# Causal masks written first into their PSUM banks, two query blocks sharing a bank, in the forgetting attention of a hybrid trunk

## The chip, the core and the metric

The kernel runs on one core of one Trainium2 chip. A core has five engines, each with its own in-order queue: TensorE (PE, with the weight load shown as PEld), VectorE (DVE), ScalarE (ACT), GpSimd (POOL) and SyncE (SP), which issues the DMAs. TensorE writes to PSUM, which has eight banks of 512 float32 columns on each of 128 partitions; VectorE and ScalarE read it there. The metric is the device time of one execution in microseconds (us), lower is better. A difference of about 0.2% (4.7 us) is what a measurement of this kernel can tell from no change.

## The reference

The reference is a two-layer trunk on 1024 frames of 1024 channels: a layer of forgetting attention (FoX), a layer of gated linear attention, each followed by a SwiGLU. The change touches the attention only:

```python
log_f = jax.nn.log_sigmoid(f_logit + b_f)
cum = jnp.cumsum(log_f, axis=1).transpose(0, 2, 1)
for blk in range(S // Q_BLOCK):                      # 8 blocks of 128 queries
    qs, qe = blk * Q_BLOCK, (blk + 1) * Q_BLOCK
    logits = jnp.einsum('bqhd,bkhd->bhqk', q[:, qs:qe], k[:, :qe]) * scale
    logits = logits + cum[:, :, qs:qe, None] - cum[:, :, None, :qe]
    mask = (qs + jnp.arange(Q_BLOCK))[:, None] >= jnp.arange(qe)[None, :]
    p = jax.nn.softmax(jnp.where(mask, logits, -inf), axis=-1)
    outs.append(jnp.einsum('bhqk,bkhd->bqhd', p, v[:, :qe]))
```

There are 16 heads of 64 channels. Query block qb attends to the first (qb + 1) * 128 keys, and the causal mask cuts only the last 128 of them, the diagonal block.

## The kernel before, in words

The attention works on pairs of heads p = 0 to 7, in each on a head a = 0 or 1, and in each head on four pairs of query blocks, g = 0 to 3, in the order `ORDER = (0, 3, 1, 2)`; query block qb is 2g + qi. `scores(u)` computes one such unit (p, a, g). It cuts the keys of a query block into pieces of at most 512 columns: one piece for qb 0 to 3 (128, 256, 384 and 512 wide), and two for the others (384 + 256, 512 + 256, 512 + 384, 512 + 512). That makes 12 pieces and 8 masks a head.

For each piece TensorE writes two matmuls into a PSUM tile: `Qs` with `K1` (L1260) and `Qs` with `KL` (L1261), in which float32 operands are split in a high and a low part. The piece that ends on the diagonal gets a third one (L1263), 128 columns wide: the bfloat16 identity times `maskb`, a constant block, which adds the mask. VectorE then reads the piece out of PSUM (L1266), adds the cumulated gates, writes it to the tile `lp` and keeps the running minimum of each row in `st`; a second piece starts from the first one's minimum. ScalarE takes the exponential of the whole row and its sum (L1270), VectorE the reciprocal (L1271), GpSimd multiplies (L1272).

The PSUM tiles of the pieces come from a ring of two banks, `sr`, b0 and b1 in turn (`sr, tr, orr, pj = ps_rings(2, 3, 1, 2)`). A piece can be written only when VectorE has read the piece that had its bank before.

`outputs` then transposes the probabilities on TensorE (L1292, tiles `t`), ScalarE and VectorE split them in a high and a low part (L174, L175, tiles `pt`), and TensorE multiplies with V (L1304, L1306, tiles `o`). A unit's `outputs` follows the next unit's `scores`. `weave` interleaves all that with the projections of the next head pair (tiles `qk` and `vps`, L305 to L307), or in the last pair with the output projection (`fo`), by the costs that each step yields. A scheduler then fixes each engine's order when the program is built, and adds the waits; the engines run in that order. VectorE also computes parts of the conditioning vector there (tiles `acc0`, L503 and L505), whose weights come by DMA.

## Time and profile before

| what | value |
|---|---|
| median of 3 runs | 2363.45 us (2361.98 to 2363.59) |
| span of the profiled execution | 2360.5 us, from its first to its last instruction |
| time of the profiled execution outside its span | not listed; its span lies 2.95 us below the median of the runs |
| attention, all of its score pieces | about 97 us to 605 us of the span |
| TensorE busy | 2339.7 us, 99% of the span |
| mean granted TensorE clock | 0.994 |

The rows shown below give for each group of instructions or for each run of equal instructions a start in the span, a duration, the engine, the line of the kernel, the operation, and its output and inputs; at the end, in brackets, how long the engine sat idle before it and what ended that. The duration of a matmul is its time from start to end in a pipeline: what it takes from TensorE's time is the distance from its start to the next one's start. A weight load (PEld) runs beside the matmul before it.

### The profile page before, as it was taken

How to read it: one execution, taken by the hardware profiler on the slowest of the kernel's cores; microseconds unless marked ns; L12 is line 12 of the kernel's file. 1: busy time of each engine (PE TensorE's matmuls, PEld its weight loads, DVE VectorE, ACT ScalarE, POOL GpSimd, SP SyncE). 2: the span in 40 equal slices, each digit the busy share in tenths (PEclk: the TensorE clock that was granted, in tenths of full speed). 3: DMA queues.
4: the chain of work that ended last, by engine and by line, in shares of the span. 5: the costliest groups of instructions: out<-in, count | busy, mean ns of one | idle time of the engine just before them, and what ended most of it. 6: DMA issues, size and time to landing. Idle time of an engine off the chain costs nothing. (4 is left out here: it accounts for less than half of the span.)

```text
span 2360.5 us, 35758 instructions
## 1 busy us (share of the span) xinstructions
PE 2339.7 (99%) x12208; PEld 1992.7 (84%) x12208; DVE 1791.0 (76%) x2996; ACT 1122.5 (48%) x2186; POOL 1101.5 (47%) x993
## 2 busy tenths in 40 slices
PE   8999999999999999999999999999999999999999
PEld 7888888888888888888888898898888888888888
DVE  6578787886688888885788765668787777876787
ACT  6556566575453343345324644444453433345326
POOL 1334444533355666653363531345446665643262
PEclk8999999999999999999999999999999999999999
DMA  8423333332435545457665543554434544457664
GB/s 265 145 79 113 105 121 95 121 126 99 134 100 173 189 161 170 159 185 259 225 224 170 147 130 93 148 180 169 143 114 163 165 152 147 157 197 259 227 198 150
DMA packets 348719, 375.00 MB, mean 159 GB/s; under 512 B 25500, under 2 KB 286776, under 8 KB 348536
## 3 DMA queue, kind: packets, MB, share of 16 engines
q1 hardware_dynamic: 348536, 372.72, 48.2%
q8 instruction: 96, 1.57, 0.3%
q14 instruction: 87, 0.71, 0.1%
HBM read 275.56 MB, written 97.06 MB: 158 GB/s over the span
## 5 line engine op out<-in xcount | busy, mean ns | idle before, releaser
L175 DVE TENSOR_TENSOR o_s<-xv_s,o_s 128x512 fp32r<-128x512 f32 (+1 forms) x376 | 322.4, 862 | 54.5 <-ACT o_s L174 52.9
L174 ACT CAST o_s<-xv_s 128x512 fp32r<-128x512 f32 (+1 forms) x376 | 216.9, 587 | 290.5 <-PE p_b L307 239.1
L307 PE MATMUL p_b<-B,o_s 128*128 128x512 f32 x608 | 236.0, 389 | 0.0
L305 PE MATMUL p_b<-B,o_s 128*128 128x512 f32 x608 | 235.6, 390 | 0.4 <-DVE x L1637 0.4
L306 PE MATMUL p_b<-B,o_s 128*128 128x512 f32 x608 | 235.9, 389 | 0.0
L918 POOL TENSOR_TENSOR ex_s<-xv_s,xv_s 128x512 f32<-128x512 f32 (+1 forms) x64 | 90.5, 1414 | 285.1 <-DMA xv_s<-in_ffn_w_in_dram 118.8
L1272 POOL TENSOR_SCALAR lp_s<-lp_s,st 128x128 f32<-128x128 f32 (+7 forms) x128 | 98.1, 770 | 246.3 <-DVE st L1271 230.7
L305 PE MATMUL p_b<-T,o_s 128*128 128x512 f32 x480 | 186.9, 389 | 0.0
L306 PE MATMUL p_b<-T,o_s 128*128 128x512 f32 x480 | 186.8, 389 | 0.0
L307 PE MATMUL p_b<-T,o_s 128*128 128x512 f32 x480 | 181.2, 389 | 0.0
L305 PEld LDWEIGHTS p_b<-B,o_s 128*128 128x128 f32 x608 | 114.1, 188 | 24.5 <-DVE x L1637 1.0
L307 PEld LDWEIGHTS p_b<-B,o_s 128*128 128x128 f32 x608 | 114.1, 188 | 23.9
L306 PEld LDWEIGHTS p_b<-B,o_s 128*128 128x128 f32 x608 | 114.1, 188 | 23.5
L1270 ACT ACTIVATE lp_s<-lp_s,st 128x128 f32<-128x128 f32 (+7 forms) x128 | 99.4, 777 | 59.7 <-DVE st L1266 58.6
L920 POOL TENSOR_TENSOR xv_s<-ex_s,xv_s 128x512 f32<-128x512 f32 (+1 forms) x64 | 87.4, 1366 | 62.3 <-DVE o_s L175 60.0
L174 ACT CAST pt_s<-t_b 128x512 fp32r<-128x512 f32 (+1 forms) x160 | 79.7, 547 | 72.0 <-PE t_b L1292 71.4
L1637 DVE TENSOR_TENSOR ex_s<-ex_s,p_b 128x512 f32<-128x512 f32 x140 | 93.7, 681 | 19.6 <-PE p_b L307 19.5
L175 DVE TENSOR_TENSOR pt_s<-t_b,pt_s 128x512 fp32r<-128x512 f32 (+1 forms) x160 | 96.3, 630 | 15.7 <-ACT pt_s L174 15.1
L307 PEld LDWEIGHTS p_b<-T,o_s 128*128 128x128 f32 x480 | 90.1, 188 | 18.7
L305 PEld LDWEIGHTS p_b<-T,o_s 128*128 128x128 f32 x480 | 90.1, 188 | 18.6
L306 PEld LDWEIGHTS p_b<-T,o_s 128*128 128x128 f32 x480 | 90.1, 188 | 18.6
L246 POOL TENSOR_TENSOR w_l_s<-w__s,w_h_s 128x256 fp32r<-128x256 f32 x90 | 69.6, 801 | 76.7 <-ACT w_h_s L242 58.8
(1801 smaller groups left out, 7440.8 us busy)
## 6 DMA issues: line engine op xcount, KB each, us to landing
xv_s<-in_ffn_w_in_dram SPq DMA_DIRECT2D x176, 256.0 KB, 3.2
hid_B<-x SPq DMA_DIRECT2D x70, 512.0 KB, 2.9
ad_s<-in_ada_w_dram SPq DMA_DIRECT2D x384, 64.0 KB, 2.4
hid_T<-x SPq DMA_DIRECT2D x36, 512.0 KB, 2.9
xv_s<-in_ffn_w_out_dram SPq DMA_DIRECT2D x96, 192.0 KB, 5.0
ada_s<-in_ada_w_dram SPq DMA_DIRECT2D x96, 128.0 KB, 2.8
xv_s<-in_ffn_w_out_dram SPq DMA_DIRECT2D x40, 256.0 KB, 2.9
T2o<-hid_T SPq DMA_DIRECT2D x18, 512.0 KB, 8.5
```

Of the source, the lines that this page charges most:

```text
L174: nc.scalar.copy(hi, src)
L175: nc.vector.tensor_sub(lo, src, hi.bitcast(F32))
L246: (nc.gpsimd if i < 3 else nc.vector).tensor_sub(lo[:, cs], rw[:, cs], hi[:, cs].bitcast(F32))
L305: nc.tensor.matmul(ps, ah, bh, start=start, stop=False, skip_group_check=chain)
L306: nc.tensor.matmul(ps, ah, bl, start=False, stop=False, skip_group_check=chain)
L307: nc.tensor.matmul(ps, al, bh, start=False, stop=stop, skip_group_check=chain)
L918: nc.gpsimd.tensor_add(s1, a21, a22)
L920: nc.gpsimd.tensor_sub(a11, s1, a11)
L1270: nc.scalar.activation(lp, lp, AF.Exp, bias=mcur, scale=-1.0, accum_out=st[:, qi, 2:3])
L1272: nc.gpsimd.tensor_scalar(lp, lp, st[:, qi, 3:4], 1.0, op0=ALU.mult, op1=ALU.mult)
L1637: nc.vector.tensor_add(d, d if src is None else dest(G, src), ps)
```

## The change

In `scores`, the mask is now the first matmul into its PSUM tile, with `start=True`, and the pieces accumulate onto it. It is issued by a helper, `masks`, a piece by `piece`, and the exponential and what follows by `exps`. What the four pairs of query blocks do now:

- g = 0: one bank holds both query blocks (128 and 256 columns). One mask matmul of 256 columns, in two blocks at columns 0 and 256, is written first, then the piece of qb 0, then that of qb 1.
- g = 1: two banks as before; both masks stand in the program ahead of the first piece.
- g = 2: the first 384 columns of qb 4 as before; then one bank for the last 256 columns of qb 4 and the last 256 of qb 5, with one mask matmul of 256 columns ahead; then the first 512 columns of qb 5. So the two pieces of qb 5 are in the opposite order.
- g = 3: the same pieces as before, with the masks ahead of the second ones.

A head now has 6 mask matmuls in place of 8 (96 in place of 128 in all), 10 banks in place of 12, and the same 12 pieces. No transfer is added or removed; in the built order of SyncE's queue seven short stretches of DMA issues within the attention differ.

```diff
--- before.py
+++ after.py
@@ -1249,27 +1249,74 @@
         else:
             lps = [lpr([P, (2 * g + 1 + i) * P], F32, f"lp{p}{a}{g}{i}") for i in range(2)]
         st = sm.tile([P, 2, 4], F32, tag="st", bufs=4, name=f"st{p}{a}{g}")
-        for qi in range(2):
+        least = [[], []]
+
+        def masks(ps, at):
+
+            o_, m_ = ps[:, at[0]:at[0] + P], maskb
+            if len(at) == 2:
+                o_ = ps.rearrange("p (a b) -> p a b", b=at[1] - at[0])[:, :, at[0]:at[0] + P]
+                m_ = maskb.unsqueeze(1).to_broadcast([P, 2, P])
+            nc.tensor.matmul(o_, identb, m_, start=True, stop=False, skip_group_check=True)
+
+        def piece(ps, c0, qi, k0, k1, masked, last):
+
             qb = 2 * g + qi
-            qs, lp, Wd, mcur = psl(qb), lps[qi], (qb + 1) * P, 3e38
-            cuts = (0, 384, 640) if Wd == 640 else (0, Wd) if Wd <= HALF else (0, HALF, Wd)
-            for n_, (k0, k1) in enumerate(zip(cuts, cuts[1:])):
-                ps = sr([P, k1 - k0], F32, f"s{p}{a}{qb}{k0}")
-                early = u == (0, 0, 0)
-                diag = k1 == Wd
-                nc.tensor.matmul(ps, Qs[:, qs], K1[:, k0:k1], start=True, stop=False)
-                nc.tensor.matmul(ps, Qs[:, qs], KL[:, k0:k1], start=False, stop=not diag)
-                if diag:
-                    nc.tensor.matmul(ps[:, k1 - k0 - P:], identb, maskb, start=False, stop=True)
-                mnew = st[:, qi, n_:n_ + 1]
-                with tc.issue_after(v_last) if early else ExitStack():
-                    nc.vector.tensor_tensor_reduce(lp[:, k0:k1], ps, cm[:, k0:k1], 1.0, mcur,
-                                                   ALU.add, ALU.min, mnew)
-                mcur = mnew
-                yield max(0.22, 0.00085 * (k1 - k0))
-            nc.scalar.activation(lp, lp, AF.Exp, bias=mcur, scale=-1.0, accum_out=st[:, qi, 2:3])
+            o_, qs = ps[:, c0:c0 + k1 - k0], psl(qb)
+            nc.tensor.matmul(o_, Qs[:, qs], K1[:, k0:k1], start=not masked, stop=False, skip_group_check=masked)
+            nc.tensor.matmul(o_, Qs[:, qs], KL[:, k0:k1], start=False, stop=last, skip_group_check=masked)
+            got = least[qi]
+            mnew = st[:, qi, len(got):len(got) + 1]
+            with tc.issue_after(v_last) if u == (0, 0, 0) else ExitStack():
+                nc.vector.tensor_tensor_reduce(lps[qi][:, k0:k1], o_, cm[:, k0:k1], 1.0, got[-1] if got else 3e38,
+                                               ALU.add, ALU.min, mnew)
+            got.append(mnew)
+            return max(0.22, 0.00085 * (k1 - k0))
+
+        def exps(qi):
+            lp = lps[qi]
+            nc.scalar.activation(lp, lp, AF.Exp, bias=least[qi][-1], scale=-1.0, accum_out=st[:, qi, 2:3])
             nc.vector.reciprocal(st[:, qi, 3:4], st[:, qi, 2:3])
             nc.gpsimd.tensor_scalar(lp, lp, st[:, qi, 3:4], 1.0, op0=ALU.mult, op1=ALU.mult)
+
+        def bank_(n, nm):
+            return sr([P, n], F32, f"s{p}{a}{g}{nm}")
+
+        if g == 0:
+            ps = bank_(HALF, "")
+            masks(ps, (0, 256))
+            yield piece(ps, 0, 0, 0, P, True, False)
+            exps(0)
+            yield piece(ps, P, 1, 0, 2 * P, True, True)
+            exps(1)
+        elif g == 1:
+            p0, p1 = bank_(3 * P, 0), bank_(4 * P, 1)
+            masks(p0, (2 * P,))
+            masks(p1, (3 * P,))
+            yield piece(p0, 0, 0, 0, 3 * P, True, True)
+            exps(0)
+            yield piece(p1, 0, 1, 0, 4 * P, True, True)
+            exps(1)
+        elif g == 2:
+            ps = bank_(3 * P, 0)
+            yield piece(ps, 0, 0, 0, 3 * P, False, True)
+            ps = bank_(HALF, "")
+            masks(ps, (P, 3 * P))
+            yield piece(ps, 0, 0, 3 * P, 5 * P, True, False)
+            exps(0)
+            yield piece(ps, 2 * P, 1, 4 * P, 6 * P, True, True)
+            ps = bank_(HALF, 1)
+            yield piece(ps, 0, 1, 0, HALF, False, True)
+            exps(1)
+        else:
+            for qi in range(2):
+                ps = bank_(HALF, 2 * qi)
+                yield piece(ps, 0, qi, 0, HALF, False, True)
+                n_ = (3 + qi) * P
+                ps = bank_(n_, 2 * qi + 1)
+                masks(ps, (n_ - P,))
+                yield piece(ps, 0, qi, HALF, HALF + n_, True, True)
+                exps(qi)
         return lps
 
     def outputs(u, lps):
```

The lines of the mask and of the two matmuls of a piece are L1260, L1266 and L1267 in the changed kernel, VectorE's read is L1271, the reciprocal L1279, the transposes L1339, the products with V L1351 and L1353.

The scheduler's order of the two programs is the same before the attention and, apart from line numbers, after it on all five engines. In the order of the kernel before, 108 of the 128 masks are followed by a matmul with float32 weights that isn't a transpose, and 20 by a transpose. In that of the changed kernel all 96 are followed by such a float32 matmul, none by another mask (so the two masks of g = 1 don't stand side by side in TensorE's queue), and 19 of them come directly after a transpose.

The first place is TensorE's queue at the start of the third head pair (p = 2). `s2000` and `s2010` are the score tiles of qb 0 and qb 1 of the kernel before, `s200` is the shared one and `s2030` the next unit's first; `b0` and `b1` are the banks, `qk031` is a projection. Before:

```order
L1260 MATMUL s2000_b0_49_2479<-KA2_1690,QA2_1688 128x128 [waits DVE_49]
L1261 MATMUL s2000_b0_49_2479<-KLA2_1692,QA2_1688 128x128
L1263 LDWEIGHTS identb_72
L1263 MATMUL s2000_b0_49_2479<-maskb_84,identb_72 128x128
L305 MATMUL qk031_b7_18_2594<-h0h5_187,w384_h_s23_17_1953 128x512
L306 MATMUL qk031_b7_18_2594<-h0l5_188,w384_h_s23_17_1953 128x512
L307 MATMUL qk031_b7_18_2594<-h0h5_187,w384_l_s24_18_1954 128x512
L1260 MATMUL s2010_b1_50_2507<-KA2_1690,QA2_1688 128x256 [waits DVE_49]
L1261 MATMUL s2010_b1_50_2507<-KLA2_1692,QA2_1688 128x256
L1263 LDWEIGHTS identb_72
L1263 MATMUL s2010_b1_50_2507<-maskb_84,identb_72 128x128
```

In the changed kernel:

```order
L1260 LDWEIGHTS identb_72
L1260 MATMUL s200_b0_41_2463<-maskb_84,identb_72 128x2x128 [waits DVE_49]
L1266 MATMUL s200_b0_41_2463<-KA2_1682,QA2_1680 128x128
L1267 MATMUL s200_b0_41_2463<-KLA2_1684,QA2_1680 128x128
L305 MATMUL qk031_b7_18_2576<-h0h5_187,w384_h_s23_17_1943 128x512
L306 MATMUL qk031_b7_18_2576<-h0l5_188,w384_h_s23_17_1943 128x512
L307 MATMUL qk031_b7_18_2576<-h0h5_187,w384_l_s24_18_1944 128x512
L1266 MATMUL s2030_b1_42_2560<-KA2_1682,QA2_1680 128x512 [waits DVE_49]
L1267 MATMUL s2030_b1_42_2560<-KLA2_1684,QA2_1680 128x512
L1266 MATMUL s200_b0_41_2463<-KA2_1682,QA2_1680 128x256 [waits DVE_49]
L1267 MATMUL s200_b0_41_2463<-KLA2_1684,QA2_1680 128x256
```

One mask of 256 columns stands ahead of both pieces; the 512-column piece of the next unit has moved ahead of qb 1's piece, which now waits for VectorE (to have read qb 0's piece out of the same bank), and the mask itself carries the wait for the bank.

The second place is VectorE's queue at the end of the fifth head pair (p = 4), between the reads of qb 4 and those of qb 5 (tiles `lp4121`, `st412`). Before:

```order
L505 SCALAR_TENSOR_TENSOR acc0_s25_1_749<-ada043_s18_48_5093,c42_164,acc0_s25_1_749 128x256 [waits DMAHW6_49,DMAHW7_49,DMAHW1_49,DMAHW0_49]
L175 TENSOR_TENSOR pt4110_s51_96_4823<-t4110_b4_96_4818,pt4110_s51_96_4823 128x512 [waits Activation_49]
L505 SCALAR_TENSOR_TENSOR acc0_s25_1_749<-ada043_s18_48_5093,c42_164,acc0_s25_1_749 128x256 [waits DVE_49]
L1271 RECIPROCAL st412_4760<-st412_4760 128x1 [waits Activation_49]
L505 SCALAR_TENSOR_TENSOR acc0_s25_1_749<-ada043_s18_48_5093,c42_164,acc0_s25_1_749 128x256 [waits DVE_49]
L175 TENSOR_TENSOR pt4111_s48_97_4830<-t4111_b2_97_4826,pt4111_s48_97_4830 128x384 [waits Activation_49]
L1266 ISA lp4121_s47_63_4759,st412_4760<-s4150_b0_119_4803,cum9_s44_10_4058 128x512 [waits PE_49,Pool_49]
L1266 ISA st412_4760 128x1
L505 SCALAR_TENSOR_TENSOR acc0_s25_1_749<-ada043_s18_48_5093,c42_164,acc0_s25_1_749 128x256 [waits DVE_49]
L1321 TENSOR_TENSOR oT4_s52_5_4203<-o413_b5_38_4674,ot413_4755 64x256 [waits Activation_49]
L1266 ISA lp4121_s47_63_4759,st412_4760<-s415512_b1_120_4807,cum9_s44_10_4058,st412_4760 128x256 [waits DVE_49,PE_49]
```

In the changed kernel:

```order
L505 SCALAR_TENSOR_TENSOR acc0_s25_1_749<-ada043_s18_48_5051,c42_164,acc0_s25_1_749 128x256 [waits DMAHW6_49,DMAHW1_49,DMAHW7_49,DMAHW0_49,DVE_49]
L1279 RECIPROCAL st412_4722<-st412_4722 128x1 [waits Activation_49]
L505 SCALAR_TENSOR_TENSOR acc0_s25_1_749<-ada043_s18_48_5051,c42_164,acc0_s25_1_749 128x256 [waits DVE_49]
L175 TENSOR_TENSOR pt4110_s51_96_4783<-t4110_b4_96_4778,pt4110_s51_96_4783 128x512 [waits Activation_49]
L505 SCALAR_TENSOR_TENSOR acc0_s25_1_749<-ada043_s18_48_5051,c42_164,acc0_s25_1_749 128x256 [waits DVE_49]
L175 TENSOR_TENSOR pt4111_s48_97_4790<-t4111_b2_97_4786,pt4111_s48_97_4790 128x384 [waits Activation_49]
L505 SCALAR_TENSOR_TENSOR acc0_s25_1_749<-ada043_s18_48_5051,c42_164,acc0_s25_1_749 128x256 [waits DVE_49]
L1271 ISA lp4121_s47_63_4721,st412_4722<-s412_b0_99_4727,cum9_s44_10_4026 128x256 [waits PE_49,Pool_49]
L1271 ISA st412_4722 128x1
L1271 ISA lp4121_s47_63_4721,st412_4722<-s4121_b1_100_4768,cum9_s44_10_4026,st412_4722 128x512 [waits DVE_49]
L1271 ISA st412_4722 128x1
```

The reciprocal of qb 4 has moved ahead of a split of transposed probabilities (`pt4110`) and a step of the conditioning vector (`acc0`); the reads of qb 5 have moved together, the 256-column one ahead of the 512-column one, behind all four steps of `acc0`.

## The prediction

> **What bounds the kernel now.** I read the page first, then the attention's stretch alone (busy time by window), then what TensorE waited for in it.
>
> ```profile
> span 2360.5 us, 35758 instructions
> PE 2339.7 (99%) x12208; PEld 1992.7 (84%) x12208; DVE 1791.0 (76%) x2996; ACT 1122.5 (48%) x2186; POOL 1101.5 (47%) x993
> 97.00:605.00 508.00, 502.88 (x3218) 440.72 (x3217) 378.80 (x960) 304.03 (x647) 221.85 (x316) 1.00 0.34 105
> PE t_b L1292 <- POOL lp_s L1272: 2.7, 3, 1.8
> PE qk_b L305 <- DVE QB L842: 1.1, 2, 0.5
> PE s_b L1260 <- DVE st L1266: 0.4, 2, 0.3
> ```
>
> TensorE is busy for 503 of the attention's 508 us (the columns of the third row are TensorE, its weight load, VectorE, ScalarE, GpSimd, clock). What it waits for there is small, and the longest wait, 1.8 us, is for normalised probabilities. So TensorE's own work is the bound, and a matmul taken away is worth what it takes from TensorE's time, as long as no wait fills the hole. VectorE, at 379 of 508 us, has room on average, but not everywhere (below).
>
> **What a mask costs.** The group of the masks, and the weight load of an ordinary score matmul:
>
> ```profile
> L1263 PEld LDWEIGHTS <-identb x128: 95/96/146, 97.5 to 589.5; 128*128 128x128 bf16 x128
> L1263 PE MATMUL s_b<-maskb,identb x128: 229/230/330, 97.5 to 589.5; 128*128 128x128 bf16 x128
> L1261 PEld LDWEIGHTS s_b<-KLA,QA x96: 187/189/333, 97.4 to 559.4; 128*128 128x128 f32 x96
> ```
>
> 230 ns is a latency, and isn't taken from TensorE's time. The price is in the starts. First a mask ahead of a 512-column matmul, then one ahead of 256-column ones, then one ahead of transposes, and last two transposes without a mask:
>
> ```profile
> 193.03 0.40 PE L307 MATMUL qk_b<-h0h,w_l_s 128*128 128x512 f32 x1
> 193.26 0.39 PE L305 MATMUL qk_b<-h0h,w_h_s 128*128 128x512 f32 x1
> 193.49 0.22 PE L1260 MATMUL s_b<-KB,QB 128*128 128x128 f32 x1
> 193.55 0.27 PE L1261 MATMUL s_b<-KLB,QB 128*128 128x128 f32 x1
> 193.66 0.23 PE L1263 MATMUL s_b<-maskb,identb 128*128 128x128 bf16 x1
> 193.71 0.48 PE L306 MATMUL qk_b<-h0l,w_h_s 128*128 128x512 f32 x1
> 194.02 0.40 PE L307 MATMUL qk_b<-h0h,w_l_s 128*128 128x512 f32 x1
> ...
> 183.29 0.23 PE L1263 MATMUL s_b<-maskb,identb 128*128 128x128 bf16 x1
> 183.32 0.36 PE L305 MATMUL vps_b<-wv_0h_s,h0h 128*128 128x256 f32 x1
> 183.53 0.28 PE L306 MATMUL vps_b<-wv_0l_s,h0h 128*128 128x256 f32 x1
> 183.65 0.28 PE L307 MATMUL vps_b<-wv_0h_s,h0l 128*128 128x256 f32 x1
> ...
> 179.52 0.23 PE L1263 MATMUL s_b<-maskb,identb 128*128 128x128 bf16 x1
> 179.58 0.50 PE L1292 MATMUL t_b<-ident,lp_s 128*128 128x128 f32 x3
> 179.84 0.36 PE L305 MATMUL vps_b<-wv_4h_s,h0h 128*128 128x256 f32 x1
> 180.04 0.28 PE L306 MATMUL vps_b<-wv_4l_s,h0h 128*128 128x256 f32 x1
> ...
> 211.10 0.38 PE L1292 MATMUL t_b<-ident,lp_s 128*128 128x128 f32 x2
> 211.23 0.48 PE L306 MATMUL qk_b<-h0l,w_h_s 128*128 128x512 f32 x1
> 211.55 0.40 PE L1260 MATMUL s_b<-KB,QB 128*128 128x512 f32 x1
> ```
>
> A 512-column matmul takes 0.23 us (193.03 to 193.26), a 256-column one 0.12 (183.53 to 183.65). From the mask's start to the end of the next matmul's slot it is 0.36 (193.66 to 194.02) and 0.24 (183.29 to 183.53). So a mask takes 0.13 and 0.12 us, though only 0.04 to 0.05 pass until the next start: the rest shows as a longer slot of its successor, whose 189 ns weight load doesn't fit behind so short a matmul. I take 0.125. Two transposes take 0.45 - 0.23 = 0.22 (211.10 to 211.55 with a 512-column matmul), 0.11 each. So the mask ahead of three transposes takes 0.52 - 0.33 - 0.12 = 0.07.
>
> **The change part by part.** *Masks of before.* By the built order 108 masks are followed by a float32 matmul that is no transpose and 20 by a transpose: 108 x 0.125 + 20 x 0.07 = 14.9 us of TensorE's time.
>
> *Masks of after.* 64 of 128 columns, all ahead of a float32 score matmul: 64 x 0.125 = 8.0. The 32 of 256 columns have no row. Bounds: no dearer than two masks (0.25), and no cheaper than 0.12, the slot of a 256-column float32 matmul; I take 0.12, since such a slot already hides a float32 weight load (183.53 to 183.65). 32 x 0.12 = 3.8 (to 8.0). Sum 11.8, so the edit gives 3.1 us; at the dear end, 16.0, it costs 1.1.
>
> *Masks behind transposes.* 19 masks now follow a transpose. Between 193.49 and 194.02 three 128-column matmuls (K1, KL, mask) take 0.53 - 0.23 = 0.30, though the first has the next float32 load behind it (0.11) and so has the mask (0.125): about 0.06 is left for the middle one, whose successor is the mask with its 96 ns load. A transpose ahead of a mask may likewise take 0.06 in place of 0.11: 19 x 0.05 = 0.9, between 0 and 0.9. I take 0.9. TensorE's work falls by 4.0 us (4.0 to -1.1).
>
> The Trainium skill, "TensorE: Matmul & The Clock Gate", section "Back-to-back issue gap", has about 81 ns a matmul for a stream of loads and 128-column matmuls and 262 cycles, an estimated 109 ns, for 256 columns. By it the masks would fall from 128 x 81 = 10.4 us to 64 x 81 + 32 x 109 = 8.7, a gain of only 1.7 us. The rows above, with a float32 load behind the bfloat16 matmul, are dearer than its 81 ns, and I go by them.
>
> *Pieces, reads, exponentials.* Same numbers and widths; nothing is gained or lost in work. The first mask of a piece hides nothing new: it needs only constants and a free bank, and the score matmuls behind it would have waited for that bank. The masks of g = 1 are not neighbours in the built order, so they cost what single ones do. The seven stretches of DMA issues that differ go past waiting steps of their queue; DMA is 0.34 busy in the stage (the window's eighth number), and I cost them at nothing; if weights came late, TensorE's projections would wait.
>
> *The new waits.* The second piece in a shared bank waits for VectorE to have read the first, and behind it in TensorE's queue wait projections, transposes and products with V that need nothing of it. How far VectorE lags at worst: the 384-column piece of qb 4 at the end of the fifth head pair, and its read.
>
> ```profile
> 398.88 0.34 PE L1261 MATMUL s_b<-KLB,QB 128*128 128x384 f32 x1
> ...
> 408.63 0.55 DVE L1266 CUSTOM_DVE_ANT_0 lp_s<-s_b,cum_s 128x384 f32<-128x384 f32 x1
> ```
>
> Nearly 10 us. But in the built order the second piece mostly stands several us of other matmuls behind the first; in the first place shown with the change, three 512-column projections and a pair of 512-column scores, 5 x 0.23 = 1.15 us. Tightest are the ends of the head pairs, where the next unit's mask of 256 columns follows closely on the piece that holds its bank. How it stands there before:
>
> ```profile
> 531.06 0.23 PE L1263 MATMUL s_b<-maskb,identb 128*128 128x128 bf16 x1
> 531.54 0.33 PE L1260 MATMUL s_b<-KA,QA 128*128 128x128 f32 x1 [0.25 <-DVE st L1266]
> ...
> 530.79 0.69 DVE L1266 CUSTOM_DVE_ANT_0 lp_s<-s_b,cum_s 128x512 f32<-128x512 f32 x1
> 531.94 0.47 DVE L1266 CUSTOM_DVE_ANT_0 lp_s<-s_b,cum_s,st 128x256 f32<-128x256 f32 x1
> ```
>
> TensorE there already waits for a 512-column read (0.69 us, to 531.48). Afterwards it waits for a 256-column read (0.47) that can start only when the piece itself is done. Bounds for the six ends where TensorE has next to nothing between (the second to seventh head pair): from 0 (VectorE late anyway) to the whole read, 0.47, each. What the masks save inside these few us is lost too, since the chain read, exponential, reciprocal, normalising sets when TensorE goes on. I take 0.2 us for each of six, 1.2 us, between 0 and 2.8.
>
> *The sum.* -4.0 + 1.2 = -2.8 us. It is made against the profiled execution, whose span of 2360.5 lies 2.95 us below the median of the runs (what lies around the span isn't listed, and I carry it over): 2363.45 - 2.8 = 2360.6 us. After the attention the built order is unchanged, so that part should only shift.
>
> **The rivals.** *Slower: the shared bank.* VectorE's lag, not TensorE's work, could decide at the 32 second pieces. The rule of the Trainium skill, "PSUM — Partial Sum Buffer", section "PSUM bank collisions raise a hardware error", speaks for it: guard by bank, not by address, so one engine may not read one half while another writes the other half. The built order has such a wait at every second piece; no run here shows the error. The gain is gone at 4.0 / 32 = 0.125 us a piece, and the kernel is 0.2% slower from (4.0 + 4.7) / 32 = 0.27 us. With 0.4 us, about a 256-column read, it is 12.8 - 4.0 = +8.8: 2372. Against it: TensorE's waits for these reads (L1260 on L1266) are 0.4 us in all today.
>
> *Faster: the longest wait goes as well.* At the end of the fifth head pair TensorE stands still, and just afterwards runs at half clock:
>
> ```profile
> 412.04 0.23 PE L1263 MATMUL s_b<-maskb,identb 128*128 128x128 bf16 x1
> 414.09 0.55 PE L1292 MATMUL t_b<-ident,lp_s 128*128 128x128 f32 x3 [1.82 <-POOL lp_s L1272]
> ...
> 415.50:418.90 3.40, 3.40 (x16) 3.04 (x15) 2.81 (x10) 2.11 (x6) 1.09 (x2) 0.51 0.85 260
> ```
>
> The transposes wait for qb 4's probabilities. The built order moves the reciprocal that they need ahead of a split and a step of `acc0`, which should shorten the wait by about half. If wait and half clock (3.4 x 0.49 = 1.7 us) both went, that would be 1.8 + 1.7 = 3.5 us more than the 4.0: 2363.45 - 7.5 = 2356. Against it: the reads of qb 5 are now behind all four steps of `acc0`, and the mask of the next unit waits for one of them.
>
> *Nothing: the gain is swallowed.* If VectorE's chain sets the pace for the last third of each head pair, or if the merged mask costs as much as two, what TensorE saves comes back as waiting: between -1 and +2 us, say 2364.
>
> **How the numbers follow.** The forecast, 2360.6, has its own bounds at -4.0 (no new wait) and -0.3 (waits of 2.8 and no gain behind transposes): 2359.4 to 2363.1; since starts are read to 0.01 us, the price of 128 masks may be off by 1.3 us besides. It gets 0.35, the faster rival 0.27, the slower 0.23, nothing 0.15. Faster by over 0.2% (below 2358.7): 0.27 and 0.09 of the forecast, 0.36. Slower (above 2368.2): 0.23. Within: 0.26 of the forecast and the 0.15, 0.41. The range goes from 2355.5, the faster rival, to 2367.5, the lower part of the slower one; some 0.2 is left out, mostly above.
>
> **What would show it.** In the changed profile: 96 masks, the start distances of a merged mask and its successor together about 0.12 us above that successor's own slot; attention's stretch 2 to 4 us shorter and the rest unchanged; TensorE's waits on L1271 of some 1 us in all, at the ends of the head pairs. I am wrong if these waits reach 4 us, if the merged mask takes 0.2 us, or if half-clock stretches come or go.

## The result, and the profile after

The changed kernel takes 2371.93 us (median of 5 runs, 2369.98 to 2372.3) beside 2363.45 us (2361.82 to 2365.68): a ratio of 1.0031, 95% interval 1.002 to 1.0041, so 0.3% slower, by some 8 us. The forecast was 2360.6 and the range ended at 2367.5.

The first lines of the page of the changed kernel: span, then each engine's busy time, share of the span and instructions.

```profile
span 2370.5 us, 35659 instructions
PE 2342.6 (99%) x12176; PEld 1992.7 (84%) x12176; DVE 1788.6 (75%) x2996; ACT 1121.0 (47%) x2186; POOL 1101.1 (46%) x993
```

TensorE has 32 matmuls fewer and is busy 2.9 us longer. The busy share, 99% in both, shows nothing: a matmul at half clock counts as busy, and the waits that matter are a few us. So the stages were compared by starts of the same matmuls in two profiled executions of each kernel (the second ones are runs of the next section). "Attention" goes from the first score or mask matmul to the last product with V; the "head loop" is the stage of the gated linear attention from the first transpose of a finished output (tile `ogt`) to the first matmul of the output projection (tile `oc`). The last row is the time of the profiled execution itself.

| us | before | before, again | after | after, again |
|---|---|---|---|---|
| attention | 507.2 | 506.2 | 510.6 | 508.3 |
| from there to the head loop | 764.5 | 763.9 | 766.3 | 765.4 |
| head loop | 246.8 | 246.9 | 251.3 | 255.6 |
| from there to the end | 744.7 | 745.0 | 744.6 | 746.1 |
| time of the execution | 2362.3 | 2362.2 | 2372.3 | 2375.6 |

Between the means of the two pairs, the attention is 2.8 us longer, the way to the head loop 1.7, the head loop 6.6, the remainder 0.5 (11.6 in all; these four executions lie further apart than the medians, which differ by 8.5). About half of the loss (4.5 of 10.0 us between the first profiles, 6.6 of 11.6 between the means) lies in a stage that the change doesn't touch, 765 us behind it.

**In the attention.** TensorE's queue around a merged mask and, further on, around another one (start, duration, engine, line, operation):

```profile
192.69 0.28 PE L1260 MATMUL s_b<-maskb,identb 128*128 128x256 bf16 x1
192.72 0.31 PE L1266 MATMUL s_b<-KB,QB 128*128 128x128 f32 x1
192.87 0.28 PE L1267 MATMUL s_b<-KLB,QB 128*128 128x128 f32 x1
...
216.01 0.28 PE L1260 MATMUL s_b<-maskb,identb 128*128 128x256 bf16 x1
216.05 0.36 PE L1266 MATMUL s_b<-KB,QB 128*128 128x256 f32 x1
216.25 0.28 PE L1267 MATMUL s_b<-KLB,QB 128*128 128x256 f32 x1
216.37 0.40 PE L306 MATMUL qk_b<-h0l,w_h_s 128*128 128x512 f32 x1
```

From the merged mask to the end of its successor's slot pass 216.25 - 216.01 = 0.24 us, and the 256-column matmul behind takes 0.12: the merged mask costs 0.12 us, as much as one of 128 columns. (At all 17 places where a merged mask stands ahead of a 256-column matmul the two take 0.23 to 0.24 us.) To separate work from standing still, I gave every matmul between the two ends of the attention the usual distance to the next start for its kind between such neighbours (the 35th percentile over all traces of this study) and called the remainder stalls (what half clock costs is among them). Before: 490.6 us of work and 16.6 and 15.6 of stalls. After: 486.8 and 23.8 and 21.4. By this estimate TensorE's work fell by 3.7 us, and stalls took back 4.8 to 8.2. Its size hangs on which neighbours are counted: by the shape of the matmul before alone the work falls by 2.6 us, by the shapes of both neighbours by 5.4. That stalls grew holds in each.

What TensorE waited for in the changed kernel's attention (waiter, releaser: us in total, times, longest), and then how long its clock was halved; the columns of the last rows are TensorE, weight load, VectorE, ScalarE, GpSimd, granted clock, DMA share, GB/s:

```profile
PE t_b L1339 <- POOL lp_s L1280: 1.6, 2, 1.0
PE s_b L1260 <- DVE st L1271: 1.4, 3, 0.6
PE o_b L1353 <- DVE oT_s L1368: 1.3, 4, 0.4
PE qk_b L305 <- DVE QB L842: 1.2, 2, 0.7
PE o_b L1353 <- DVE pt_s L175: 1.1, 3, 0.5
PE s_b L1266 <- DVE st L1271: 0.6, 2, 0.3
PE t_b L1339 <- DVE pt_s L175: 0.5, 2, 0.4
```

```profile
415.50:418.90 3.40, 3.06 (x9) 2.04 (x8) 2.62 (x9) 1.91 (x6) 1.02 (x2) 0.50 0.92 290
476.90:480.30 3.40, 2.95 (x8) 2.38 (x9) 1.54 (x7) 0.87 (x4) 1.85 (x4) 0.50 0.38 141
1514.60:1518.00 3.40, 3.40 (x9) 2.65 (x9) 3.40 (x8) 1.52 (x4) 0.00 (x0) 0.50 0.31 90
```

The one long wait of before (1.8 us for normalised probabilities) is shorter, 1.0. Beside it are many short ones, so that the seven rows make 7.7 us together, where the kernel before has 4.7: for reads of scores, for split probabilities, for outputs. Two stretches at half clock are new, one in the attention and one in the head loop. Where the delay begins is seen on ScalarE, whose exponential waits for VectorE's read, in the kernel before and then in the changed one:

```profile
ACT lp_s L1270 <- DVE st L1266: 58.6, 64, 2.8
```

```profile
ACT lp_s L1278 <- DVE st L1271: 80.9, 65, 4.0
```

The reads come later against ScalarE, 80.9 us of waits in place of 58.6, and all that follows a read (exponential, reciprocal, normalising, transpose, split) comes later too.

**In the head loop.** VectorE's and TensorE's queues at the same place, before:

```profile
1500.56 1.01 DVE L505 SCALAR_TENSOR_TENSOR ad_s<-ad_s,c 128x256 f32<-128x256 f32 x2 [5.49 <-DMA ad_s<-in_ada_w_dram]
1502.06 1.01 DVE L505 SCALAR_TENSOR_TENSOR ad_s<-ad_s,c,ad_s 128x256 f32<-128x256 f32 x2 [0.49 <-DMA ad_s<-in_ada_w_dram]
1502.98 0.69 DVE L2068 TENSOR_TENSOR gy_s<-gk_b,ei_s 128x512 f32<-128x512 f32 x1
1503.58 0.68 DVE L2069 TENSOR_TENSOR t_s<-gk_b,t_s 128x512 f32<-128x512 f32 x1
...
1503.14 0.60 PE L2098 MATMUL kdt_b<-ident,t_s 128*128 128x128 f32 x4
1504.75 0.27 PE L307 MATMUL at_b<-gq20h_s,kil_s 128*128 128x128 f32 x1
1504.86 0.45 PE L305 MATMUL gr_b<-h1h,w_h_s 128*128 128x512 f32 x1
```

and after:

```profile
1508.81 1.36 DVE L505 SCALAR_TENSOR_TENSOR ad_s<-ad_s,c 128x256 f32<-128x256 f32 x2 [6.25 <-DMA ad_s<-in_ada_w_dram]
1510.27 1.63 DVE L505 SCALAR_TENSOR_TENSOR ad_s<-ad_s,c,ad_s 128x256 f32<-128x256 f32 x2
1511.83 0.68 DVE L2115 TENSOR_TENSOR gy_s<-gk_b,ei_s 128x512 f32<-128x512 f32 x1
1512.43 0.68 DVE L2116 TENSOR_TENSOR t_s<-gk_b,t_s 128x512 f32<-128x512 f32 x1
...
1508.88 0.60 PE L2145 MATMUL kdt_b<-ident,t_s 128*128 128x128 f32 x4
1510.50 0.27 PE L307 MATMUL at_b<-gq20h_s,kil_s 128*128 128x128 f32 x1
1513.16 0.50 PE L305 MATMUL gr_b<-h1h,w_h_s 128*128 128x512 f32 x1 [2.39 <-DVE t_s L2116]
```

VectorE's steps of the conditioning vector (L505, tile `ad`) wait for a transfer of their weights, and the products with the projection (L2115, L2116), which TensorE needs, stand behind them in the queue. Before, VectorE goes on 2.58 us ahead of the transposes at 1503.14, its products are done before TensorE needs them, and TensorE waits for nothing. After, it goes on 0.07 us ahead of the same transposes, 2.5 us later; TensorE waits 2.39 us, and from 1.4 us after that runs at half clock for 3.4 us. All that TensorE waited for in the head loop, before and after:

```profile
PE kdt_b L2098 <- DVE kdl_s L175: 0.2, 1, 0.2
```

```profile
PE gr_b L305 <- DVE t_s L2116: 2.4, 1, 2.4
PE at_b L306 <- DVE gq10l_s L175: 0.4, 1, 0.4
PE kdt_b L2145 <- DVE kdl_s L175: 0.2, 1, 0.2
```

2.8 us more of waiting and 3.4 x 0.50 = 1.7 us lost to the clock are the 4.5 us by which the loop grew.

### The profile page after: what moved, and what is told of

Read it like the earlier page. It is cut to its first block, busy times and chain, and to the rows that moved or that the text cites. A ratio compares the mean times of both kernels' runs of the same rounds, so it can differ in the third digit from the quotient of the medians.

```text
span 2370.5 us, 35659 instructions
## 1 busy us (share of the span) xinstructions
PE 2342.6 (99%) x12176; PEld 1992.7 (84%) x12176; DVE 1788.6 (75%) x2996; ACT 1121.0 (47%) x2186; POOL 1101.1 (46%) x993
## 5 line engine op out<-in xcount | busy, mean ns | idle before, releaser
L1278 ACT ACTIVATE lp_s<-lp_s,st 128x128 f32<-128x128 f32 (+7 forms) x128 | 99.3, 776 | 85.5 <-DVE st L1271 80.9
L307 PEld LDWEIGHTS p_b<-B,o_s 128*128 128x128 f32 x608 | 114.1, 188 | 23.8
L306 PEld LDWEIGHTS p_b<-B,o_s 128*128 128x128 f32 x608 | 114.2, 188 | 23.5
L930 POOL TENSOR_TENSOR xv_s<-xv_s,xv_s 128x512 f32<-128x512 f32 x40 | 53.8, 1345 | 108.7 <-issue 69.2
```

The source lines that it names most:

```text
L306: nc.tensor.matmul(ps, ah, bl, start=False, stop=False, skip_group_check=chain)
L307: nc.tensor.matmul(ps, al, bh, start=False, stop=stop, skip_group_check=chain)
L930: nc.gpsimd.tensor_sub(r[A12], r[A12], r[A11])
L1278: nc.scalar.activation(lp, lp, AF.Exp, bias=least[qi][-1], scale=-1.0, accum_out=st[:, qi, 2:3])
```

## The experiments

Ratios are to runs of the kernel before on the same chip, taken between the others; 0.001 is 2.4 us. Stages are those of the table above.

### The change once more

Nothing is edited.

> The changed kernel once more, for a second profile. In its first profile the attention (first mask or score matmul to last product with V) takes 511 us against 507 before, and what follows it 1757 us against 1750, though the built order there is the same. If the second part is a property of the program (theory: the attention's new waits put the rest into a worse alignment with the loads of the conditioning weights), both numbers repeat within 1 us, with the 2.4 us wait near 1512 us and half clock behind it. If it is chance of one execution (rival), the attention repeats and the rest falls anywhere between 1750 and 1757 us.

2375.57 us in one run. Attention 508.3, head loop 255.6, and stretches at half clock in the head loop alone (from 1430.6 and 1515.9). What TensorE waited for in that loop:

```profile
PE gr_b L305 <- DVE t_s L2116: 3.0, 1, 3.0
PE at_b L305 <- ACT gq10h_s L174: 2.3, 1, 2.3
PE at_b L306 <- DVE gq10l_s L175: 0.4, 1, 0.4
```

Neither expectation held: the attention didn't repeat (508.3 after 510.6), and what follows it took more than in the first profile. The stretches at half clock inside the attention aren't a lasting mark of the change, the loss in the head loop is. One profile of a stage is good to some 2 us in the attention and some 4 in the loop.

### Which part of the change

Masks first, but every piece in a bank of its own and 128 masks:

```diff
         if g == 0:
-            ps = bank_(HALF, "")
-            masks(ps, (0, 256))
-            yield piece(ps, 0, 0, 0, P, True, False)
-            exps(0)
-            yield piece(ps, P, 1, 0, 2 * P, True, True)
-            exps(1)
+            for qi in range(2):
+                n_ = (1 + qi) * P
+                ps = bank_(n_, qi)
+                masks(ps, (n_ - P,))
+                yield piece(ps, 0, qi, 0, n_, True, True)
+                exps(qi)
...
         elif g == 2:
...
-            ps = bank_(HALF, "")
-            masks(ps, (P, 3 * P))
+            ps = bank_(2 * P, 1)
+            masks(ps, (P,))
...
```

> Masks first, but no bank shared: 8 masks and 12 banks a head, pieces in the order of before. Theory (shared banks make TensorE wait): nothing to wait for anew, attention 506 to 509 us, time within 2 us of before unless the rest shifts. Rival (putting the mask first is what costs, since it is no longer followed by transposes or since the bank is asked for earlier): attention 510 us or more, time 4 us or more above before.

2365.79 us (10 runs), ratio 1.0004 [0.9994, 1.0013]. Attention 507.9, work 489.4, stalls 18.5.

The same, but qb 0 and qb 1 share a bank and a mask as in the changed kernel:

```diff
         if g == 0:
-            for qi in range(2):
-                n_ = (1 + qi) * P
-                ps = bank_(n_, qi)
-                masks(ps, (n_ - P,))
-                yield piece(ps, 0, qi, 0, n_, True, True)
-                exps(qi)
+            ps = bank_(HALF, "")
+            masks(ps, (0, 256))
+            yield piece(ps, 0, 0, 0, P, True, False)
+            exps(0)
+            yield piece(ps, P, 1, 0, 2 * P, True, True)
+            exps(1)
```

> Masks first, only qb 0 and 1 share a bank and a mask (112 masks). TensorE's work falls by 16 x 0.12 = 2 us. Theory: the wait of qb 1's piece and of the merged mask at the ends of the head pairs comes with this half of the change and eats its 2 us: attention 507 to 509 us. Rival (the sharing in g = 2 does it): attention 505 us, the 2 us gained.

2371.86 us (7 runs), ratio 1.0034 [1.0022, 1.0045]. Attention 511.0, work 487.5, stalls 23.5. That is longer than either expectation, and the time is that of the whole change; but its head loop took only 248.0 us, and against the means of before 6.6 us of the loss lie in the attention and on the way to the head loop.

The same as the first, but with the shared bank and the reversed pieces of g = 2 as in the changed kernel:

```diff
-            ps = bank_(2 * P, 1)
-            masks(ps, (P,))
-            yield piece(ps, 0, 0, 3 * P, 5 * P, True, True)
+            ps = bank_(HALF, "")
+            masks(ps, (P, 3 * P))
+            yield piece(ps, 0, 0, 3 * P, 5 * P, True, False)
             exps(0)
-            ps = bank_(HALF, 2)
+            yield piece(ps, 2 * P, 1, 4 * P, 6 * P, True, True)
+            ps = bank_(HALF, 1)
             yield piece(ps, 0, 1, 0, HALF, False, True)
-            ps = bank_(2 * P, 3)
-            masks(ps, (P,))
-            yield piece(ps, 0, 1, 4 * P, 6 * P, True, True)
             exps(1)
```

> Masks first, only qb 4 and 5 share a bank and a mask, with qb 5's pieces in the changed order (112 masks). TensorE's work falls by 2 us. Theory: at the ends of the head pairs the next unit's first mask waits for qb 5's last read and TensorE's waits there grow by some 4 us: attention 508 to 510 us. Rival (g = 0 does it): attention 505 us.

2368.54 us (10 runs), ratio 1.0013 [1.0003, 1.0023]. Attention 508.0, work 488.3, stalls 19.7.

Two more split these again. In the first qb 0 and qb 1 share a bank, but each has its own mask of 128 columns, just ahead of its piece:

```diff
         if g == 0:
             ps = bank_(HALF, "")
-            masks(ps, (0, 256))
-            yield piece(ps, 0, 0, 0, P, True, False)
+            masks(ps, (0,))
+            yield piece(ps, 0, 0, 0, P, True, True)
             exps(0)
+            masks(ps, (256,))
             yield piece(ps, P, 1, 0, 2 * P, True, True)
             exps(1)
```

> Only qb 0 and qb 1 share a bank (as in the run that shared for g = 0 alone: 2371.9 us, attention 511.0), but with a mask of 128 columns of its own ahead of each piece, 128 masks. Theory that sharing the bank, which puts both reads behind one another before the bank is free, is what costs: 16 x 0.12 = 1.9 us of TensorE's time more than that run, 2372 to 2375, attention 511 to 514. Rival that the early merged mask is what costs (it keeps the second piece's half of the bank from being written by anything else, and comes before both pieces): back to the run without sharing, 2366 to 2368, attention 508 to 509.

2367.38 us (10 runs), ratio 1.0018 [1.0008, 1.0027]. Attention 510.3, work 489.6, stalls 20.7.

In the second only g = 2 shares, with the 512 columns of qb 5 in the program ahead of the second piece in the shared bank:

```diff
             exps(0)
-            yield piece(ps, 2 * P, 1, 4 * P, 6 * P, True, True)
-            ps = bank_(HALF, 1)
-            yield piece(ps, 0, 1, 0, HALF, False, True)
+            p1 = bank_(HALF, 1)
+            yield piece(p1, 0, 1, 0, HALF, False, True)
+            yield piece(ps, 2 * P, 1, 4 * P, 6 * P, True, True)
             exps(1)
```

> Only g = 2 shares its bank, and the 512 columns of qb 5 stand in the program ahead of the second piece of the shared bank, as in the kernel before. Theory that the reversed order of qb 5's two pieces puts VectorE's reads together and the longer read last, behind which exponential, reciprocal and transposes wait: 2 to 3 us faster than the run that shared for g = 2 with the reversed order (2368.5), so 2366, attention 506 to 507. Rival that the shared bank costs by itself: 2368 to 2371, since the bank is held longer still.

2365.66 us (10 runs), ratio 1.0017 [1.0007, 1.0028]. Attention 507.4, work 488.6, stalls 18.8.

Against the first run the estimate of the work falls by 1.9 us with 16 merged masks for g = 0, as priced, and by 1.1 with those for g = 2 (by the shapes of both neighbours, by under 1 us each). The stalls rise with what ScalarE waits for VectorE's reads. The row of that wait, in the run with no shared bank and in the four that share one (g = 0; g = 0 with two masks; g = 2; g = 2 with the 512 columns first):

```profile
ACT lp_s L1278 <- DVE st L1271: 67.3, 63, 3.8
```

```profile
ACT lp_s L1278 <- DVE st L1271: 80.6, 63, 4.0
```

```profile
ACT lp_s L1278 <- DVE st L1271: 85.0, 70, 3.5
```

```profile
ACT lp_s L1278 <- DVE st L1271: 74.0, 65, 3.2
```

```profile
ACT lp_s L1278 <- DVE st L1271: 69.4, 68, 3.4
```

Masks written first raise it from 58.6 to 67.3 and cost nothing that the time shows. Sharing for qb 0 and qb 1 raises it to the 81 of the changed kernel or above, and the attention of both profiles is 2 to 3 us longer than without sharing, with a merged mask or with two. That points at the shared bank rather than the mask, and doesn't show it: two profiles of the changed kernel lie 2.3 us apart in the attention. In the run with two masks TensorE's waits of over 0.15 us come to 5.7 us beside 5.6 without sharing, and what its attention has more is mostly a further stretch at half clock (1.7 us); with the merged mask they come to 10.5. Neither expectation for the run with two masks holds as written, since its attention (510.3) lies nearer to the first and its total (2367.4) in the second. For g = 2 the total doesn't tell the two orders of qb 5's pieces apart, but with the 512 columns first ScalarE waits hardly longer than without sharing. The totals of these runs also hold the head loop, of which the next sections tell that a us or two ahead of it can cost several there; they don't sort the parts by themselves.

### What the masks are worth at most, and the yardstick

The kernel before once more:

> The kernel before once more, as a yardstick. Ratio 1.000 +- 0.001. In the profiles so far the part after the attention (from the last product with V to the end) took 1750.2 us in the one profile of before and 1753.6 to 1761.5 us in five profiles of changed kernels, though its order is the same in all. Theory that this part varies from execution to execution (by some us, in the gated-linear-attention stage, 247 to 256 us from its first product to its last projection): here it comes out at 1752 to 1758, so 2 to 8 us above the first profile. Rival, that the change itself lengthens that part: here it is again within 1 us of 1750.

2363.29 us (10 runs), ratio 0.9995 [0.9986, 1.0005]; the part after the attention, here and in what was expected counted to TensorE's last matmul, 5.8 us before the span ends, took 1750.1 us. That speaks against a random loss: both profiles of before have a head loop of 247 us, both of the changed kernel one of 251 or more. Both executions lie 0.5 to 3 us under the medians of before in the later runs, though, so a loop of 247 is not the longest that before can have.

The kernel before without masks, so that its attention is no longer causal:

```diff
-                nc.tensor.matmul(ps, Qs[:, qs], KL[:, k0:k1], start=False, stop=not diag)
-                if diag:
-                    nc.tensor.matmul(ps[:, k1 - k0 - P:], identb, maskb, start=False, stop=True)
+                nc.tensor.matmul(ps, Qs[:, qs], KL[:, k0:k1], start=False, stop=True)
```

> Leaves the 128 masks out of the kernel before (its attention is then not causal): measures what all mask matmuls are worth together. Theory that TensorE's work bounds the attention and a mask costs 0.125 us ahead of a float32 matmul and 0.07 ahead of a transpose: attention shorter by 14.9 us where nothing else fills the hole, 2349 us. Rival that VectorE's chain at the ends of the head pairs and the conditioning loads behind it take back what TensorE saves: 2355 to 2360. Rival that a mask costs only the 0.04 us to the next start: 5 us, 2359.

2357.55 us (6 runs), ratio 0.9971 [0.9958, 0.9983], 6.9 us faster. TensorE's work in the attention fell by 15.5 us (490.6 to 475.1; the rows of the prediction price the 128 masks at 14.9), stalls grew from 16.6 to 24.9 and the attention became 7.2 us shorter. So the price of a mask agrees, and the exchange was not one for one: when TensorE is relieved of all 128 masks, half of it comes back as stalls. Its waits of over 0.15 us for VectorE rise from 2.0 to 8.1 us, those for GpSimd fall from 2.7 to 1.0. The middle expectation, that VectorE's chain takes back part, comes nearest.

### The head loop without its transfers

In both kernels the conditioning weights of the second layer's parts 2 to 4 are loaded only once each (15 of 16 groups of transfers a part are left out, and VectorE's steps use the first group again, so the result is another):

```diff
             n = steps.popleft()
+            if (l, j) in ((1, 2), (1, 3), (1, 4)) and kept:
+                got.append(kept[0])
+                return
             raw = raw_of([P, nt * 256], F32, f"ada{l}{j}{n}").rearrange("p (t c) -> p t c", t=nt)
             ada_load(raw, l, j, n, nt)
             got.append(raw)
+            kept.append(raw)
```

> Kernel before, but the conditioning weights of the second layer's parts 2 to 4 are loaded only once each (15 of 16 transfers left out, VectorE's 96 steps stay and use the first piece), so VectorE can't wait for those transfers in the gated-linear-attention stage. Theory that this stage's varying length comes from VectorE's wait for them (28 to 32 us of waits in all profiles): stage (first product to last projection, 247 us before) falls to 240 or less, total 2355 to 2360. Rival that those waits are hidden: within 2 us of 2363.5.

> The same edit in the changed kernel. Theory (attention and the part up to the head loop lose 2 to 4 us, the other 5 us are VectorE's wait for those transfers): 2 to 4 us slower than the kernel before with the same edit, part after the attention within 1.5 us of that kernel's. Rival (the extra 5 us after the attention have another cause): still 7 to 9 us slower.

2365.25 us, ratio 1.0005 [0.9996, 1.0014], and 2366.2 us, ratio 1.0006 [0.9997, 1.0016] (10 runs each). The loss of the change is gone: by the ratios the two differ by 0.0001, by the medians by 1 us. Their head loops take 248.8 and 248.7 us, and TensorE waits there for one and the same thing, in the kernel before and in the changed one:

```profile
PE go_b L306 <- DVE S_t L175: 0.9, 1, 0.9
```

Two parts of the expectations missed. The loop of before didn't get shorter but 2 us longer; and the difference is 1 us rather than 2 to 4, with an attention of 508.8 against 507.7. The edit also leaves the scheduler with other work: from 1328 to 1659 us of the span, so all through the head loop, TensorE's queue differs from that of the kernels with all transfers in 60 stretches and VectorE's in 53, alike in both kernels. So these two runs don't tell whether it is the missing transfers or the other order that makes the loops equal.

### Both chains relieved

Besides, VectorE does only one in four of the 96 steps of `acc0` in the attention:

```diff
-                for t in range(nt):
+                for t in range(nt if ahead else 1):
```

> The kernel before with the conditioning weights of the second layer's parts 2 to 4 loaded once, as above, and with VectorE doing only one in four of the 96 steps of acc0 in the attention (72 steps of 0.485 us left out, 35 us of VectorE's time; their transfers stay). Theory that VectorE's queue at the ends of the head pairs makes TensorE stand still: TensorE's stalls in the attention fall from 16.6 us to about 12, attention from 507.7 to some 503 us, total some 2360. Rival that the stalls come from the banks or from the order alone: attention 507 to 508, total within 2 us of 2365.

> The same two edits in the changed kernel. Theory that VectorE's steps took back what TensorE saved: the gain that was forecast appears, attention 2 to 4 us shorter than that of the kernel before with the same edits, total 2 to 4 us lower. Rival that a shared bank itself makes TensorE wait for VectorE's read, with or without those steps: attention 1 to 3 us longer than that of the kernel before with the same edits, total as much higher.

2363.49 us, ratio 1.0001 [0.9991, 1.001], and 2363.66 us, ratio 1.0004 [0.9993, 1.0016] (10 runs each). Attentions of 505.2 and 504.8 us, stalls of 14.6 and 17.9. The forecast gain doesn't appear even here, and no loss either: of 3.7 us of TensorE's work 3.3 go into stalls. The order of the queues in the attention is another here too. The steps of `acc0` are probably part of what makes TensorE wait (against the kernels with the first edit alone, 17.1 to 14.6 us of stalls before, 22.0 to 17.9 after; one profile each), but neither theory was right about the remainder.

### A pure delay

Is it the changed attention that lengthens the head loop, or only that the stages before it have moved? Into the kernel before I put a delay: the first 512-column matmul of qb 6 of one unit is written 15 or 8 more times, 0.23 us each. No other row of any queue changes.

```diff
+                for _ in range(15 if u == (3, 0, 3) and qb == 6 and k0 == 0 else 0):
+                    nc.tensor.matmul(ps, Qs[:, qs], K1[:, k0:k1], start=True, stop=True)
                 nc.tensor.matmul(ps, Qs[:, qs], K1[:, k0:k1], start=True, stop=False)
```

> Kernel before with the first 512-column score matmul of qb 6 (p = 3, first head) written 15 times more into the same bank, nothing else changed in any queue: a pure delay of TensorE of 15 x 0.23 = 3.45 us in the middle of the attention. Theory that the part after the attention is a tight chain of VectorE and transfers that comes out longer when the stages before it are shifted: part after the attention 1753 to 1758 us in place of 1750, total 2369 to 2374, as the changed kernel's. Rival that a delay only shifts it: part after the attention 1750 +- 1, total 2363.5 + 3.5 = 2367. A third way, the stalls at the ends of the later head pairs swallow the delay: attention under 508, total 2364 to 2365.

> The same with 8 more matmuls, 1.84 us. Theory of the tight chain: part after the attention 1752 to 1758, total 2367 to 2372, not in proportion to the delay. Rival (only shifted): part after it 1750 +- 1, total 2365.3.

2372.09 us (4 runs), ratio 1.0039 [1.0023, 1.0055], for 3.45 us of delay; 2368.46 us (10 runs), ratio 1.0028 [1.0018, 1.0037], for 1.84 us. That is some 9 and 6 us (by the intervals 5 to 13 and 4 to 9): 4 to 6 us more than was put in. Both attentions are longer by about the delay (510.1 and 508.1), both head loops take 251.2 us. TensorE's waits in the loop, with 8 matmuls, and the row of a stretch at half clock there:

```profile
PE gr_b L305 <- DVE t_s L2071: 1.3, 1, 1.3
PE at_b L305 <- ACT gq10h_s L174: 0.8, 1, 0.8
PE at_b L306 <- DVE gq10l_s L175: 0.4, 1, 0.4
```

```profile
1511.30:1514.70 3.40, 3.40 (x10) 2.63 (x9) 3.40 (x7) 1.63 (x5) 0.52 (x1) 0.51 0.27 77
```

They are the waits of the changed kernel, in a kernel whose attention wasn't changed but for the delay.

A delay of the same length with fewer instructions, two plain float32 matmuls in place of eight (four on the engine; K1 to KL takes 1.95 us in the trace in place of 0.24, a delay of 1.7 us), and the 15 matmuls in the kernel whose transfers are left out:

```diff
+                for _ in range(2 if u == (3, 0, 3) and qb == 6 and k0 == 0 else 0):
+                    nc.tensor.matmul(ps, Qs[:, qs].bitcast(F32), K1[:, k0:k1].bitcast(F32), start=True, stop=True)
```

> A delay of TensorE at the same place of the kernel before, but by two matmuls of 512 columns in plain float32, which go through the array in several passes: estimated at four times 0.23 us, 1.8 us in all, as long as the 8 extra matmuls of the run before (2368.5, part after the attention 1757.9), with 2 instructions in place of 8. Theory that the delay itself lengthens the part after the attention: 2366 to 2371, that part 1753 to 1758. Rival that the shifted positions in TensorE's instruction stream do it: 2364.5 to 2366, that part 1750 to 1752.

> The 15 extra matmuls (3.45 us; alone they cost 9.3 us, 2372.1) in the kernel before whose conditioning weights of parts 2 to 4 are loaded once (2365.3 without the delay). Theory that the excess over the delay is VectorE's chain with these transfers: only the delay is left, 2368 to 2369.5, part after the attention 1751 to 1753. Rival that the excess has another cause: 2373 to 2375, that part 1755 to 1758.

The short one: 2368.7 us (10 runs), ratio 1.0019 [1.001, 1.0028], 4.5 us for 1.7. Its profiled execution is one of the shortest of its runs (2366.65) and has a loop of 247.0, so the excess stands in the times and not in that trace: by the time the first expectation holds, by the part after the attention (1751.8) its rival. The one without transfers: 2368.98 us (10 runs), ratio 1.002 [1.001, 1.0029], so 0.0015 or 3.5 us (to within some 3) above the kernel with the same edit and no delay: what was put in. Its loop takes 248.7 us. The part after the attention, 1755.8, is longer than was expected and in the rival's range; the excess in that profile lies before and behind the loop.

And the 15 matmuls in the changed kernel:

> The same 15 matmuls in the changed kernel. If the length of the part after the attention depends on when it is reached, it comes out elsewhere than at 1756.6 and 1761.5 (some 1750 to 1756), and the total is less than 3.45 us above 2371.9: 2368 to 2373. Rival, that the part after the attention is longer in the changed kernel whenever it is reached: 1756 to 1762, total 2374 to 2377.

2372.74 us (4 runs), ratio 1.0045 [1.0028, 1.0063]; loop 251.8, part after the attention 1756.4. By the ratios it is 3.3 us slower than without the delay, by the medians of different calls 0.8. A loop that has grown already doesn't seem to grow further, but the interval doesn't decide between the two expectations.

The head loop of all profiled executions, in us:

| kernels | head loop |
|---|---|
| before, two executions | 246.8, 246.9 |
| before, delayed (1.7, 1.84, 3.45 us) | 247.0, 251.2, 251.2 |
| before without masks | 249.8 |
| masks first, in parts (the five runs, in the order told) | 249.6, 248.0, 252.6, 250.7, 249.0 |
| changed, two executions, and delayed | 251.3, 255.6, 251.8 |
| without the transfers: five executions of both kernels, one delayed | 248.8, 248.7, 248.8, 248.8, 248.7 |

Without the transfers, and in the order that goes with that, the loop takes the same time to 0.1 us, whatever comes before it. With them it takes 247 to 256. What varies is TensorE's waits and its clock alone: less its waits of over 0.15 us and half of the time at half clock, the loop comes to 246.2 to 246.8 us in all fourteen executions with the transfers, and to 247.8 in the five without.

## Why the prediction was wrong

- **A mask's price: right.** The merged mask was to cost 0.12 us and costs that. TensorE's work was to fall by 4.0 us; by the estimate above it fell by 3.7 (2.6 to 5.4 by other counts). The 81 ns of the Trainium skill, "TensorE: Matmul & The Clock Gate", "Back-to-back issue gap", are not borne out where a float32 weight load follows: 120 ns.
- **"A matmul taken away is worth what it takes from TensorE's time": half right.** The condition that went with it, "as long as no wait fills the hole", is what failed. Of the 15.5 us of all masks only 7.2 reached the attention's end, and of the 4.0 us of this change none: the attention grew by 2.8. TensorE busy 99% of the time doesn't mean that its neighbours have room.
- **The new waits: wrong in size and in place.** Six ends of head pairs at 0.2 us, 1.2 us in all, were costed. The waits for VectorE's reads of scores came to 1.4 + 0.6 = 2.0 us (2.6 in the second profile), not far off. But the stalls of all kinds grew by 4.8 to 8.2 us, since a later read makes exponential, normalising, transposes and split later. The prediction named that chain for what the masks save, and counted only its first link. How much of these stalls each link makes isn't shown.
- **"After the attention the built order is unchanged, so that part should only shift": the step that failed most.** This part was put at nothing because its order stays; it was 4.5 and 8.7 us longer in the head loop alone. The same queues don't give the same time, where VectorE's queue waits for transfers and TensorE needs what stands behind them within 3 us: in the traces all of it is TensorE waiting for VectorE or ScalarE, and the half clock after that.
- **The rivals.** The slower one gave 2372 by 0.4 us at each of 32 second pieces; the time came out at 2372, but not by that mechanism, whose waits are 2.0 us in all. The rule of the Trainium skill, "PSUM — Partial Sum Buffer", "PSUM bank collisions raise a hardware error", guard by bank, may have pointed at the right part: the profiles with a shared bank for qb 0 and qb 1 have attentions longer by 2 to 3 us. The faster one was right that the wait at 412 us shortens (1.8 to 1.0), but the half clock behind it stayed in that profile. That the gain is swallowed, with some 2364 us, is what the kernels without those transfers show, 2365.25 and 2366.2; in the kernel as changed the head loop comes on top.
- **What would show it.** New half-clock stretches were named as a sign of being wrong, and two came; one of them lay in the head loop, outside the part that the prediction had costed.

Open remains why a shift by 2 us puts the loop out of step: it isn't simply later or earlier, since a kernel whose attention ends only 1 us later than before (the one that shares for g = 2) had a loop of 252.6 us, and two that end 3 and 5 us later (the short delay; the one that shares for g = 0) had loops of 247.0 and 248.0. That the transfers cause it is argued from the order of waits in the traces; the run without them has another order and doesn't settle it. Nor do the profiles divide the remaining cost of the attention cleanly between the shared bank and VectorE's other work, and the 1.7 us on the way to the head loop weren't followed.

## What to carry to other kernels

Before pricing a change on the bounding engine, look through the stages after it for a queue that waits for transfers just in time, and ask what a shift of one or two us would do there: here it cost 4.5 and 8.7 us in the two profiles, where the change was to save 2.8. A pure delay, the same matmul written a few times more with all queues unchanged, measures that in one run, and helps to tell a loss that a change makes from one that a mere shift can make. An edit that takes transfers away may give the scheduler another order, so compare the queues before reading such a run. And a bank shared by two pieces saves masks but puts VectorE's read of the first ahead of the second piece; count the whole chain behind a late read, not only TensorE's wait for it.

## What the runs showed of the hardware

- A delay of 1.84 us of one engine cost 6 us, of 3.45 us 9 us, and 3.5 us once 45 of 48 groups of transfers were left out, which also changed the order of the queues. In the two profiles with a head loop of 251.2 us the excess there is 2.7 and 3.0 us of waits and 1.7 us of half clock.
- Waits of 1.3 us (of 1510.41, with 8 matmuls) and 2.4 us (to 1513.16, changed kernel) were followed by 3.4 us at half clock (0.51 and 0.50), 0.9 and 1.4 us after TensorE had gone on. The Trainium skill, "TensorE: Matmul & The Clock Gate", "What's actually happening", has the clock halved after at least one idle window of about 3.4 us, and the window running freely. The length of the stretches agrees (3.4 us each); that a whole idle window is needed does not: no idle stretch that long stands ahead of them.
- A bfloat16 mask of 256 columns costs TensorE no more than one of 128 ahead of a float32 matmul: 0.12 us, in both cases mostly as a longer slot of its successor.
